# One decoder layer in split float32: cache copies in pieces, Sqrt for the inverse roots, sigmoids at another place, and all twelve heads of q in one pass over x

## The chip, the cores and the metric

The kernel runs on one core of a Trainium2 chip, as one launch. The metric is device time in microseconds (us); lower is better. TensorE (PE in the profile) multiplies matrices, ScalarE (ACT) and VectorE (DVE) do elementwise work, GpSimd (POOL) does a little of both and issues some DMAs, and SyncE (SP) issues most DMAs. Each engine works through its own instructions in order; they meet at semaphores.

## The reference, cut to what matters

One layer of a decoder for 256 prompt tokens and 8 decoded tokens (264 columns in all), width 2048, all in float32:

```python
xn = rmsnorm(x, norm_mix_g)
z  = xn @ w_in              # u, v (768 each), q (12 heads x 64), k, v (4 x 64 each), qm (512), 3 gates x 2048
o_g = gelu(u) * gmlp_spatial(rmsnorm(gelu(v)))            # causal 128x128 mixing
o_a = sliding_window_attention(q, k, v, cache_k, cache_v) # window 128, ALiBi, sinks
o_m = memory_attention(qm, mem_k, mem_v)                  # 256 memory tokens
x = x + (sig(g0)*(o_g @ w_br_g) + sig(g1)*(o_a @ w_br_a) + sig(g2)*(o_m @ w_br_m)) @ w_out
h = causal_conv3(rmsnorm(x, norm_ffn_g) @ w_up)
x = x + (gelu(h_a) * h_b) @ w_down
y = rmsnorm(x, final_norm_g)
# also returned: the windows of keys and values, shifted by one row for the 8 decoded tokens
# (new row 127 computed, rows 0..126 copied from cache rows 1..127), memory k and v, states
```

## The kernel before

**Arithmetic.** Every float32 matrix product is made of three matmuls in a faster format: the operand x is split into `xhi` and `xlo`, each weight tile into `whi` (a cast on ACT) and `wlo` (raw minus `whi`, on DVE), and `whi*xhi + whi*xlo + wlo*xhi` is summed in PSUM. Everything is kept transposed: features on the 128 partitions, the 264 tokens along the free axis. So one matmul streams 264 columns, and the kernel has over 11,000 of them.

**Chunks.** A weight matrix is read in chunks of 256 rows (two blocks of 128) by up to 512 columns. `wload` issues the DMA on SP into a tile `raw` (four buffers), `split` makes `whi` and `wlo` (six buffers each, so three chunks), `gemm` lists the chunks as items, and `run` walks the list: it splits one chunk ahead for the first four and two ahead afterwards, then lets the item issue its matmuls. An accumulator `acc` is one PSUM bank, four of the eight banks; the other four (`mis`) serve everything else.

**Slots.** `pump` is called once per six matmuls and advances `clock`; `at(slot, fn)` and `later(n, fn)` place other work (transposes, attention, norms) at a slot of that clock. `plan` lays out the attention, the memory attention, the gMLP branch and the convolution's state by slots counted from its start (`p(slot, ...)`). `InOrder` ties each engine's instructions into the order in which they are recorded, so this order is what an engine executes.

**The start.** x is loaded as eight tiles `xl` (two feature blocks of 128 each). `x_parts` transposes one pair of blocks on TensorE: per block two 128x128 transposes of prompt rows and one small one of the 8 decoded rows `xs`; then `xhi` on ACT and `xlo` on DVE, scaled by the norm's gain `gT`. `x_kept` keeps the plain x (`xT`) and squares; on POOL the squares are added up into `ssum`. The q columns of `w_in` come in two passes: heads 0 to 5 (three accumulators, 384 columns, 8 chunks, a pair of x transposed in each), then heads 6 to 11 (the same 8 pairs of x again). Between them `x_norm` makes the row norm: `token_norm` sums over the partitions (`ntp`), `inv_sqrt` does the root as Exp(-0.5 Ln v) with one Newton step, `spread` puts the result back along the free axis by a diagonal tile `dg` and matmuls (`stp`). The results, `r_bc`, scale each accumulator as it is read out (`r_evac`).

**The middle.** After q come k and v of the window attention, qm, the memory's keys and values (`macc`), u, v, and the gates; `plan` starts after k and v. In it `swa_plan` ends with `kv_shift`, which issues on POOL three DRAM to DRAM copies: the convolution's state, and the shifted rows of the two window caches, 1016 KB each, as one DMA each. `mem_plan` has the softmax of the memory attention (tiles `p_`, `mpT`) and for the 8 decoded tokens products on POOL (`mvc` times `pTs`). `gates` applies Sigmoid two slots after each pair of accumulators. `gmlp_plan` has the Gelus and a root.

**Activation tables.** Before an ACT function that the loaded table does not hold, an ACT_TABLE_LOAD stands in ACT's order. In the kernel before there are 16. The last stands in the final norm, between Ln and Exp.

**The end.** After the last `w_down` chunk the final norm's sums are taken (`nt`), `inv_sqrt` gives `ry`, and the rows of y, already transposed, are scaled and stored.

Of the kernel before, what the change touches and what calls it, by code (L numbers as in the profile page):

```python
# [60 lines left out]
def body(ctx, tc, x_prompt, x_sample, cache_swa_k, cache_swa_v, cache_mem_k, cache_mem_v, state_conv,  # L61
# [13 lines left out]
    psM = ctx.enter_context(tc.tile_pool(name="psM", bufs=4, space=PSUM))  # L75
# [4 lines left out]
    def mis_t(name="mis"):  # L80
        return psM.tile([128, 512], F32, name=name, tag="mis")
# [22 lines left out]
    def inv_sqrt(dst, v, shape):  # L104

        y = sm.tile(shape, F32, name="rs_y", tag="rs_y%d" % shape[1], bufs=2)
        t = sm.tile(shape, F32, name="rs_t", tag="rs_t%d" % shape[1], bufs=2)

        def a():
            S.activation(y, v, AF.Ln)  # L110
            S.activation(y, y, AF.Exp, scale=-0.5)

        def b():
            V.scalar_tensor_tensor(out=t, in0=y, scalar=-0.5, in1=y, op0=mul_, op1=mul_)
            V.tensor_tensor(t, t, v, op=mul_)
            V.scalar_tensor_tensor(out=dst, in0=t, scalar=1.5, in1=y, op0=add_, op1=mul_)
        return a, b

    def token_norm(srcs, out):

        st = {}

        def a():
            tp = st["tp"] = mis_t("ntp")
            for tb in range(3):
                np_ = 128 if tb < 2 else 8
                for i, q in enumerate(srcs):
                    T.matmul(tp[:np_, tb:tb + 1], lhsT=q[:, 128 * tb:128 * tb + np_], rhs=ones[:, 0:1],
                             start=i == 0, stop=i == len(srcs) - 1)
            v = st["v"] = sm.tile([128, 3], F32, name="nv_", tag="nv_", bufs=2)  # L130
            G.memset(v, 1.0)

        def b():
            tp, v = st["tp"], st["v"]
            V.tensor_scalar(v[:, 0:2], tp[:, 0:2], 1.0 / D, EPS, op0=mul_, op1=add_)
            V.tensor_scalar(v[:8, 2:3], tp[:8, 2:3], 1.0 / D, EPS, op0=mul_, op1=add_)
            st["f"] = inv_sqrt(out, v, [128, 3])
            st["f"][0]()
        return a, b, lambda: st["f"][1]()

    def spread(r, dst):

        st = {}

        def a():
            dg = st["dg"] = sm.tile([128, NT], F32, name="dg", tag="sq", bufs=4)
            V.tensor_scalar(dg[:, 0:128], ident, r[:, 0:1], None, op0=mul_)
            V.tensor_scalar(dg[:, 128:256], ident, r[:, 1:2], None, op0=mul_)
            V.tensor_scalar(dg[:8, 256:264], ident[:8, :8], r[:8, 2:3], None, op0=mul_)

        def b():
            tp, dg = mis_t("stp"), st["dg"]
            T.matmul(tp[:, 0:256], lhsT=ones, rhs=dg[:, 0:256], start=True, stop=True)
            T.matmul(tp[:, 256:264], lhsT=ones[:8, :], rhs=dg[:8, 256:264], start=True, stop=True)
            V.tensor_copy(dst, tp[:, :NT])
        return a, b


    ident = cst.tile([128, 128], F32, name="ident")
    make_identity(nc, ident)  # L160
    ones = cst.tile([128, 128], F32, name="ones")
    G.memset(ones, 1.0)
    warm = cst.tile([128, 1], F32, name="warm")
    S.activation(warm, ones[:, 0:1], AF.Ln)
# [10 lines left out]
    rx = cst.tile([128, 3], F32, name="rx")  # L175
# [5 lines left out]
    R, M, held = {}, {}, {}  # L181
    st_ld, st_mix, st_pb, st_me, st_gt, st_s2, st_s2p, st_s3k, st_s3v, st_s1, st_s5, st_mg = (
        ExitStack() for _ in range(12))


    ld = st_ld.enter_context(tc.tile_pool(name="ld", bufs=1))
    xls = [ld.tile([128, 2, 256], F32, name="xl%d" % i) for i in range(8)]
    xs = ld.tile([8, D], F32, name="xs")
    gm = ld.tile([16, 128], F32, name="gm")
    grow = ld.tile([48, 128], F32, name="grow")  # L190

    def x_load(i):
# [8 lines left out]
    def x_parts(k0):  # L201

        if k0 == 0:
            tp = mis_t("gtp")
            T.transpose(out=tp[:, 0:16], in_=gm, identity=ident[:16, :16])
            V.tensor_copy(gT[:, 0:16], tp[:, 0:16])
        xl = xls[k0 // 2]
        tps = []
        for j in range(2):
            kb = k0 + j  # L210
            tp = mis_t("xtp")
            js = slice(128 * j, 128 * j + 128)
            T.transpose(out=tp[:, 0:128], in_=xl[:, 0, js], identity=ident)
            T.transpose(out=tp[:, 128:256], in_=xl[:, 1, js], identity=ident)
            T.transpose(out=tp[:, 256:264], in_=xs[:, 128 * kb:128 * kb + 128], identity=ident[:8, :8])
            tps.append(tp[:, :NT])
        for j in range(2):
            S.activation(xhi[:, k0 + j, :], tps[j], AF.Copy, scale=gT[:, k0 + j:k0 + j + 1])
        for j in range(2):
            V.scalar_tensor_tensor(out=xlo[:, k0 + j, :], in0=tps[j], scalar=gT[:, k0 + j:k0 + j + 1],  # L220
                                   in1=xhi[:, k0 + j, :], op0=mul_, op1=sub_)
        return tps

    def x_kept(k0, tps):
        S.copy(xT[:, k0, :], tps[0])
        V.tensor_copy(xT[:, k0 + 1, :], tps[1])
        sq = [sm.tile([128, NT], F32, name="sq", tag="sq", bufs=4) if k0 + j else ssum for j in range(2)]
        S.activation(sq[0], tps[0], AF.Square)
        if k0 < KB - 2:
            G.tensor_tensor(sq[1], xT[:, k0 + 1, :], xT[:, k0 + 1, :], op=mul_)  # L230
        else:
            S.activation(sq[1], tps[1], AF.Square)
        E = G if k0 < KB - 2 else V
        if k0:
            E.tensor_tensor(ssum, ssum, sq[0], op=add_)
        E.tensor_tensor(ssum, ssum, sq[1], op=add_)

    def x_pair(k0):
        if k0 < KB:
            x_kept(k0, x_parts(k0))  # L240
# [12 lines left out]
    def split(load, n, pairs):  # L253
# [11 lines left out]
        for r, h, l in vs:  # L265
            S.copy(h, r)
        for r, h, l in vs:
            V.tensor_tensor(l, r, h, op=sub_)
        return list(zip(his, los))

    def run():
        chunks = [i for i, it in enumerate(items) if it[0]]
        ws, nxt, pos = {}, 0, 0
        for i, (sp, fn) in enumerate(items):
# [3 lines left out]
            look = pos + (0 if pos == 0 else 1 if pos < 4 else 2)  # L278
            while nxt < len(chunks) and nxt <= look:
                if nxt == 0:  # L280
                    wake = mis_t("wake")
                    for _ in range(5):
                        T.matmul(wake[:, 0:128], lhsT=ones, rhs=ones, start=True, stop=True)
                    x_load(0)
                    held["x"] = x_parts(0)
                    for _ in range(3):
                        T.matmul(wake[:, 0:128], lhsT=ones, rhs=ones, start=True, stop=True)
                ws[chunks[nxt]] = split(*items[chunks[nxt]][0])
                nxt += 1
                if nxt < 8:  # L290
                    x_load(nxt)
# [6 lines left out]
    def gemm(load, nkb, nm, ab, evac, pairs=False, pre=None, mid=None, banks=None):  # L298
# [3 lines left out]
        def chunk(kc):  # L302
            def mm(ws):
                if pre:
                    pre(kc)
                if kc == 0:
                    st["acc"] = banks() if banks else [acc_t() for _ in range(nm)]
                ahi, alo = ab()
                for m in range(nm):
# [9 lines left out]
                    if mid and m == 0:  # L319
                        mid(kc)  # L320
# [33 lines left out]


    def pre_q0(kc):
        if kc == 0:
            x_kept(0, held.pop("x"))
            x_pair(2)

    def open_mix():
        st_ld.close()
        R["mix"] = st_mix.enter_context(tc.tile_pool(name="mix", bufs=1))
        pb = st_pb.enter_context(tc.tile_pool(name="pb", bufs=1))
        R["kvT"] = pb.tile([128, 4, NT], F32, name="kvT")
        R["mkT"] = pb.tile([128, 4, 256], F32, name="mkT")
        R["mv_tm"] = pb.tile([128, 2, 512], F32, name="mv_tm")
        f6("qT")
        for m in range(3):
            r_evac("qT", 0, QS)(m, held[m])  # L370

    def x_norm():
        a, b, c = token_norm([ssum], rx)
        d, e = spread(rx, r_bc)
        later(1, a)
        later(2, b)
        later(5, c)
        later(5, d)
        later(8, e)
        later(9, gains)  # L380
        later(10, open_mix)

    gemm(wload(win, 1536, 384), KB, 3, xab, held.__setitem__, pairs=True, pre=pre_q0,
         mid=lambda kc: kc and x_pair(2 * kc + 2))
    act(x_norm)
    gemm(wload(win, 1536 + 384, 384), KB, 3, xab, r_evac("qT", 3, QS), pairs=True,
         banks=lambda: [acc_t(), mis_t("acc_"), mis_t("acc_")])
# [34 lines left out]
    def pre_m(kc):  # L422
# [5 lines left out]
        if kc == 6:  # L428
# [78 lines left out]

    def plan():
# [1061 lines left out]
```

## Time and profile before

| | |
|---|---|
| time, median of 3 runs | 1536.22 us (1534.65 to 1537.34) |
| the profiled execution's own time | 1537.49 us |
| its span, first to last instruction | 1535.8 us |
| busy: PE, DVE, ACT, POOL | 1512.8, 1008.1, 771.0, 156.5 us |
| mean granted TensorE clock | 0.995 of full |
| DMA | 285.82 MB, mean 186 GB/s |

Read it from PE down: PE is busy for nearly the whole span, and its busy time counts a matmul from its start to its modelled end, so that two that overlap cover the time once. A stretch in which matmuls start further apart than in the steady part is therefore the thing to look for, as well as PE's idle time. In the trace most instructions carry line L50, the helper that records them; tiles tell them apart. "xN" merges N alike instructions, and a float32 matmul counts as two.

### The profile page before, as it was taken

What the parts mean: (1) busy time and instruction counts of PE and PEld (TensorE: products, weight loads), DVE (VectorE), ACT (ScalarE), POOL (GpSimd) and SP (SyncE); (2) the same over time, 40 slices, a digit from 0 to 9 for tenths busy, and PEclk for the clock granted to TensorE, in tenths of its full rate; (3) what the DMA queues carried; (4) which work ended last, traced back from release to release, by engine and by line L of the source; (5) the groups of instructions that cost most, each with busy time, mean ns of one, the idle gap of its engine ahead of it and who ended that gap; (6) DMA issues with size and microseconds to landing.
All of it is one profiled execution on the core that took longest, in us unless ns stands there. A gap on an engine that the chain in (4) does not pass through costs nothing.

```text
span 1535.8 us, 31462 instructions
## 1 busy us (share of the span) xinstructions
PE 1512.8 (99%) x12118; PEld 1486.1 (97%) x12118; DVE 1008.1 (66%) x1926; ACT 771.0 (50%) x1481; POOL 156.5 (10%) x247
## 2 busy tenths in 40 slices
PE   9999998999999999999999999999999999999996
PEld 8997898899999999999999999999999999999996
DVE  7577695767565655766577777775444777777564
ACT  6467643556444444455555555554333555555443
POOL 5122241310000000001100000002000000000120
PEclk9999999999999999999999999999999999999998
DMA  6746697665566665555666666656556666665553
GB/s 192 220 154 206 202 315 259 200 193 178 166 183 184 183 180 179 180 180 170 185 180 179 181 184 183 180 180 186 180 183 182 183 179 179 180 179 186 179 165 109
DMA packets 154914, 285.82 MB, mean 186 GB/s; under 512 B 12140, under 2 KB 30380, under 8 KB 154716
## 3 DMA queue, kind: packets, MB, share of 16 engines
q1 hardware_dynamic: 151804, 276.30, 59.1%
q0 software_dynamic: 2960, 7.52, 1.8%
q8 instruction: 95, 1.56, 0.4%
q14 instruction: 55, 0.45, 0.1%
HBM read 279.36 MB, written 6.82 MB: 186 GB/s over the span
## 4 chain that ended last, share of the span: by engine, by line
PE 95%; DMA 2%; DVE 1%; ACT 1%; issue 1%; SPq 0%; POOLq 0%; POOL 0%; DVEq 0%; ACTq 0%
PE acc L50 87%; PE macc L50 3%; DMA raw<-in_w_in_dram 1%; PE xtp L50 1%; DVE wlo L50 1%; DMA k<-in_cache_swa_k_dram 0%; PE acc__552 L50 0%; PE acc__551 L50 0%; PE sps L50 0%; PE ov L50 0%; PE msov L50 0%; PE ptp L50 0%; ACT whi L50 0%; PE mtp L50 0%; PE ytp L50 0%
## 5 line engine op out<-in xcount | busy, mean ns | idle before, releaser
L50 DVE TENSOR_TENSOR wlo<-raw,whi 128x512 fp32r<-128x512 f32 (+1 forms) x1008 | 660.1, 697 | 478.4 <-ACT whi L50 476.2
L50 ACT CAST whi<-raw 128x512 fp32r<-128x512 f32 (+1 forms) x1008 | 564.2, 607 | 609.8 <-PE acc L50 400.2
L50 PE MATMUL acc<-xg_hi,whi 128*128 128x264 f32 x1408 | 400.4, 284 | 0.0
L50 PE MATMUL acc<-xg_lo,whi 128*128 128x264 f32 x1408 | 400.2, 284 | 0.0
L50 PE MATMUL acc<-xg_hi,wlo 128*128 128x264 f32 x1408 | 400.1, 284 | 0.0
L50 PE MATMUL acc<-xhi,whi 128*128 128x264 f32 x1152 | 337.2, 293 | 6.1 <-DVE vT L50 6.0
L50 PE MATMUL acc<-xlo,whi 128*128 128x264 f32 x1152 | 329.8, 286 | 0.4 <-DVE xlo L50 0.4
L50 PE MATMUL acc<-xhi,wlo 128*128 128x264 f32 x1152 | 329.8, 286 | 0.0
L50 PEld LDWEIGHTS acc<-xg_hi,whi 128*128 128x128 f32 x1408 | 265.5, 189 | 0.1
L50 PEld LDWEIGHTS acc<-xg_lo,whi 128*128 128x128 f32 x1408 | 265.0, 188 | 0.0
L50 PEld LDWEIGHTS acc<-xg_hi,wlo 128*128 128x128 f32 x1408 | 264.4, 188 | 0.0
L50 PEld LDWEIGHTS acc<-xhi,whi 128*128 128x128 f32 x1152 | 219.4, 190 | 10.2 <-DVE vT L50 6.2
L50 PEld LDWEIGHTS acc<-xlo,whi 128*128 128x128 f32 x1152 | 219.2, 190 | 1.3 <-DVE xlo L50 0.7
L50 PEld LDWEIGHTS acc<-xhi,wlo 128*128 128x128 f32 x1152 | 218.7, 190 | 0.2
L50 PE MATMUL acc<-ahi,whi 128*128 128x264 f32 x704 | 200.7, 285 | 0.0
L50 PE MATMUL acc<-ahi,wlo 128*128 128x264 f32 x704 | 200.1, 284 | 0.0
L50 PE MATMUL acc<-alo,whi 128*128 128x264 f32 x704 | 200.1, 284 | 0.0
L50 PEld LDWEIGHTS acc<-ahi,whi 128*128 128x128 f32 x704 | 132.7, 189 | 0.0
L50 PEld LDWEIGHTS acc<-alo,whi 128*128 128x128 f32 x704 | 132.6, 188 | 0.0
L50 PEld LDWEIGHTS acc<-ahi,wlo 128*128 128x128 f32 x704 | 132.2, 188 | 0.0
L50 DVE SCALAR_TENSOR_TENSOR t<-H,cvT,t 128x256 f32<-128x256 f32 x176 | 84.7, 481 | 3.1
L50 POOL TENSOR_TENSOR ssum<-ssum,sq 128x264 f32<-128x264 f32 x41 | 35.8, 873 | 461.8 <-ACT sq L50 459.6
(339 smaller groups left out, 1703.6 us busy)
## 6 DMA issues: line engine op xcount, KB each, us to landing
raw<-in_w_up_dram SPq DMA_DIRECT2D x176, 512.0 KB
raw<-in_w_in_dram SPq DMA_DIRECT2D x112, 512.0 KB
raw<-in_w_down_dram SPq DMA_DIRECT2D x88, 512.0 KB
raw<-in_w_in_dram SPq DMA_DIRECT2D x48, 384.0 KB
raw<-in_w_out_dram SPq DMA_DIRECT2D x32, 512.0 KB
raw<-in_w_mem_kv_dram SPq DMA_DIRECT2D x16, 512.0 KB
raw<-in_w_br_g_dram SPq DMA_DIRECT2D x12, 512.0 KB
raw<-in_w_br_a_dram SPq DMA_DIRECT2D x48, 128.0 KB
```

Of the source, the lines that this page charges most:

```text
L50: r = f(*a, **k)
```

## The change

In words, part by part:

- **q in one pass.** `q_chunk` takes all twelve heads in one walk over the pairs of x: per pair two chunks of 384 columns, six accumulators (four of `acc`, two of a pool `psX` whose other two banks serve `mis`); after q, `psX` is closed and `psM` with four banks opened. The first four half-chunks go block by block, each operand part for three heads in a row, the rest as before. The accumulators are read out on ACT with no norm; `q_norm` multiplies by `r_bc` on DVE at slots 82 and 84.
- **The start.** The 8 decoded rows are loaded as 128 rows of 128 elements (on ACT's DMA queue, like the gain `gm`) and transposed by one 128x128 transpose; a pair of x then needs four transposes and no small ones. Seven matmuls on `ones` stand first instead of five. `x_start` orders the first casts by hand; `x_pair(i)` stands at slot 5i-3.
- **Squares by fours.** `x_squares` squares four blocks in one ACT instruction and adds them on DVE in pairs; POOL adds nothing there any more.
- **Norms.** `token_norm` sums with one matmul of `ones` against `ssum` (264 columns), which leaves the sum on every partition; `spread` is gone. Roots are Sqrt on ACT, then a reciprocal on DVE and the same Newton step.
- **Cache copies.** `kv_shift` copies one cache of one decoded token, 127 KB; 16 of them stand from slot 222 to 357, nine slots apart. The state's copy stands at slot 216.
- **Sigmoids.** Those of the first group of gates stand at slots 322 to 337 of the plan, among those of the second group, after the Gelus.
- **Small shifts.** `mem_prep(0)` stands one chunk earlier, two score blocks 3 or 4 slots later, the decoded tokens' attention and memory softmax 4 slots later.

```diff
     def inv_sqrt(dst, v, shape):
         def a():
-            S.activation(y, v, AF.Ln)
-            S.activation(y, y, AF.Exp, scale=-0.5)
+            S.activation(y, v, AF.Sqrt)
         def b():
+            V.reciprocal(y, y)
             ...
+    def token_norm(src, dst):          # the old one and spread() are removed
+        def a():
+            tp = st["tp"] = mis_t("ntp")
+            T.matmul(tp[:, :NT], lhsT=ones, rhs=src, start=True, stop=True)
+        def b():
+            V.tensor_scalar(v, st["tp"][:, :NT], 1.0 / D, EPS, op0=mul_, op1=add_)
+            S.activation(dst, v, AF.Sqrt)
+        def c():
+            V.reciprocal(y, dst)
             ...
+    def x_pair(i):
+        tp = mis_t("xtp")
+        tps = [x_trans(tp[:, 256 * j:256 * j + 256], i, j) for j in range(2)]
+        for j in range(2):
+            x_hi(2 * i + j, tps[j])
+        S.copy(xT[:, 2 * i:2 * i + 2, NP_], tp.rearrange("p (j t) -> p j t", j=2))
+        for j in range(2):
+            x_lo(2 * i + j, tps[j])
+    def x_squares(g):
+        S.activation(sq, xT[:, 4 * g:4 * g + 4, :], AF.Square)
             ...
+    def q_chunk(kc, h):
+        parts = ((0, 0), (1, 0), (0, 1))
             ...
+            for w, g, m, j, (a, b) in todo:
+                o = qs["acc"][3 * g + m][:, :NT]
+                T.matmul(o, lhsT=blk(w[j][b], m), rhs=xab()[a][:, 2 * kc + j, :], start=..., stop=last)
+                if last:
+                    S.activation(R["qT"][:, 3 * g + m, :], o, AF.Copy, scale=QS)
+                if qs["n"] % 6 == 0:
+                    pump()
+    for i in range(1, 8):
+        at(5 * i - 3, lambda i=i: x_pair(i))
+    for g, slot in enumerate((14, 24, 34, 42)):
+        at(slot, lambda g=g: x_squares(g))
+    for slot, f in zip((50, 51, 54, 58), token_norm(ssum, r_bc)):
+        at(slot, f)
+    for h in range(2):
+        at(82 + 2 * h, lambda h=h: q_norm(h))
-        def kv_shift():
-            G.dma_start(o_cs[0, :, 0, :], state_conv[0, :, 1, :])
-            for src, dst in ((cache_swa_k, o_ks), (cache_swa_v, o_vs)):
-                G.dma_start(dst[0]..., src[0]...)          # 8 x 2 x 16256 elements
+        def kv_shift(src, dst, b):
+            G.dma_start(dst[0, b]..., src[0, b]...)        # 16 x 2032 elements
-        p(s + 72, kv_shift)
+        p(216, state_shift)
+        for k in range(8):
+            p(222 + 18 * k, kv_shift, cache_swa_k, o_ks, k)
+            p(231 + 18 * k, kv_shift, cache_swa_v, o_vs, k)
-                    later(2, lambda: S.activation(gt[...], gt[...], AF.Sigmoid))
+                    if gi == 0:
+                        at(plan_at[0] + 322 + 6 * br + 3 * (m // 2), sig)
+                    else:
+                        later(2, sig)
```

How the instructions stand, at three places. On PE, from its first instruction to the first product of q, before (`wake` are matmuls on `ones`, `xtp` transposes of x, `gtp` that of the gain, `acc` an accumulator):

```order
L50 MATMUL wake<-ones 128x128 x5
L50 MATMUL gtp<-ident,gm 128x16
L50 MATMUL xtp<-ident,xl_99 128x128 x2
L50 MATMUL xtp<-ident,xs 128x8
L50 MATMUL xtp<-ident,xl_99 128x128 x2
L50 MATMUL xtp<-ident,xs 128x8
L50 MATMUL wake<-ones 128x128 x3
L50 MATMUL xtp<-ident,xl_100 128x128 x2
L50 MATMUL xtp<-ident,xs 128x8
L50 MATMUL xtp<-ident,xl_100 128x128 x2
L50 MATMUL xtp<-ident,xs 128x8
L50 MATMUL acc<-xhi,whi 128x264
```

The same place in the changed kernel, up to the transposes of the second pair (`xstp` is that of the decoded rows, `xgtp` that of the gain):

```order
L50 MATMUL wake<-ones 128x128 x7
L50 MATMUL xstp<-ident,xs 128x128
L50 MATMUL xtp<-ident,xl_76 128x128 x2
L50 MATMUL xgtp<-ident,gm 128x128
L50 MATMUL xtp<-ident,xl_76 128x128 x2
L50 MATMUL wake<-ones 128x128 x3
L50 MATMUL acc<-xhi,whi 128x264 x3
L50 MATMUL acc<-xlo,whi 128x264 x3
L50 MATMUL acc<-xhi,wlo 128x264 x3
L50 MATMUL acc<-xhi,whi 128x264
L50 MATMUL acc__182<-xhi,whi 128x264
L50 MATMUL xtp<-ident,xl_77 128x128 x4
```

The second pair's transposes moved behind the first twelve products, and the small transposes are gone. On POOL, where the copies of the caches stood (- before, + changed; `mvc` are the products for the memory attention of the decoded tokens):

```order
 L50 DMA out_dram<-in_state_conv_dram 8x11264
-L50 DMA out_dram<-in_cache_swa_k_dram 8x2x16256
-L50 DMA out_dram<-in_cache_swa_v_dram 8x2x16256
 L50 MEMSET zf 128x135
 L50 MEMSET zf 128x1
-L50 TENSOR_TENSOR mvc<-mvc,pTs 128x512 x16
+L50 DMA out_dram<-in_cache_swa_k_dram 16x2032
+L50 TENSOR_TENSOR mvc<-mvc,pTs 128x512 x2
+L50 DMA out_dram<-in_cache_swa_v_dram 16x2032
+L50 TENSOR_TENSOR mvc<-mvc,pTs 128x512 x3
+L50 DMA out_dram<-in_cache_swa_k_dram 16x2032
+L50 TENSOR_TENSOR mvc<-mvc,pTs 128x512 x3
```

Two large copies ahead of the products became sixteen small ones, six of them ahead of or among the products and ten behind. On ACT, in the final norm:

```order
 L50 CAST whi<-raw 128x512 x10
 L50 ACTIVATE sq<-xT 128x264 x4
-L50 ACTIVATE rs_y<-nv__19663 128x3
-L50 ACT_TABLE_LOAD
-L50 ACTIVATE rs_y<-rs_y 128x3
+L50 ACTIVATE rs_y<-nv__19607 128x3
 L50 ACTIVATE y_tm<-y_tm,ry 128x512
```

The table load and one activation between the sums and the scaling of y are gone; over the kernel ACT has 10 table loads instead of 16.

## Rows read from the trace of the kernel before

**Rows 1.** The page's first part: busy us, share, instructions by engine.

```profile
PE 1512.8 (99%) x12118; PEld 1486.1 (97%) x12118; DVE 1008.1 (66%) x1926; ACT 771.0 (50%) x1481; POOL 156.5 (10%) x247
```

**Rows 2.** Windows: stretch, length, busy (count) by engine, PEclk, DMA share, GB/s.

```profile
240.00:250.00 10.00, 5.21 (x50) 4.26 (x48) 2.28 (x4) 1.29 (x3) 0.00 (x0) 1.00 0.90 328
250.00:260.00 10.00, 8.84 (x51) 8.84 (x52) 5.29 (x12) 3.87 (x10) 0.30 (x2) 0.66 0.63 197
...
280.00:290.00 10.00, 8.17 (x60) 7.51 (x60) 7.15 (x17) 6.50 (x14) 3.13 (x3) 1.00 0.49 152
290.00:300.00 10.00, 9.16 (x69) 8.71 (x69) 7.83 (x15) 6.86 (x14) 2.08 (x2) 1.00 0.63 197
...
400.00:450.00 50.00, 50.00 (x413) 50.00 (x412) 31.78 (x63) 21.95 (x40) 0.00 (x0) 1.00 0.59 181
```

**Rows 3.** Timeline of PE: start us, us, instruction, [idle before, releaser].

```profile
1.21 2.50 PE L50 MATMUL wake<-ones 128*128 128x128 f32 x10 [1.21 <-POOL ones L50]
...
6.05 1.65 PE L50 MATMUL wake<-ones 128*128 128x128 f32 x6
7.50 0.63 PE L50 MATMUL xtp<-ident,xl 128*128 128x128 f32 x2
...
9.08 0.59 PE L50 MATMUL acc<-xhi,whi 128*128 128x264 f32 x1
...
251.16 0.59 PE L50 MATMUL acc<-xhi,whi 128*128 128x264 f32 x1 [5.95 <-DVE vT L50]
```

**Rows 4.** The chain that ended last: start us, us, what.

```profile
9.15 5.58 PE acc L50 x24
...
18.07 0.90 PE xtp L50 x6
...
26.87 0.42 DVE wlo L50
...
37.41 0.46 PE ntp L50 x6
...
43.17 0.74 PE stp L50 x4
...
56.18 24.81 PE acc L50 x204
...
251.16 5.65 PE acc L50 x24
...
295.88 0.44 PE mptp L50 x4
...
758.63 0.94 PE stp L50 x4
```

**Rows 5.** Timeline of ACT, columns as for PE.

```profile
5.34 0.48 ACT L50 ACTIVATE xhi<-xtp,gT 128x264 fp32r<-128x264 f32 x1 [3.04 <-PE xtp L50]
...
6.56 0.92 ACT L50 CAST whi<-raw 128x384 fp32r<-128x384 f32 x2
...
248.82 1.14 ACT L50 CAST whi<-raw 128x512 fp32r<-128x512 f32 x2 [8.67 <-DMA raw<-in_w_in_dram]
...
289.90 1.28 ACT L50 ACT_TABLE_LOAD   x1 [1.04 <-DVE nm L50]
...
1524.41 1.28 ACT L50 ACT_TABLE_LOAD   x1
```

**Rows 6.** Timeline of DVE, columns as for PE.

```profile
24.04 3.25 DVE L50 TENSOR_TENSOR wlo<-raw,whi 128x384 fp32r<-128x384 f32 x4 [0.40 <-ACT whi L50]
...
40.55 1.03 DVE L50 TENSOR_TENSOR wlo<-raw,whi 128x384 fp32r<-128x384 f32 x2 [2.25 <-ACT whi L50]
```

**Rows 7.** DMA issues: what, engine, count, KB each, median us to landing.

```profile
out_dram<-in_cache_swa_k_dram POOLq DMA_DIRECT2D x1, 1016.0 KB, 11.1
```

**Rows 8.** Groups of instructions: busy us, mean ns of one, idle before.

```profile
L50 POOL TENSOR_TENSOR mvc<-mvc,pTs 128x512 f32<-128x512 f32 x16 | 18.3, 1154 | 39.4 <-DVE pTs L50 15.5 <-DMA mvc<-in_cache_mem_v_dram 14.8 <-DVE mvc L50 5.1
...
L50 POOL DMA_DIRECT2D out_dram<-in_cache_swa_k_dram x1 | 0.6, 598 | 0.0
```

More of the change, by code (lines that the diff above doesn't have):

```diff
@@ new lines, in token_norm @@
+        return a, b, c, d
+    st_ld = ExitStack()
+    ld = st_ld.enter_context(tc.tile_pool(name="ld", bufs=1, side="right"))
+    xls = [ld.tile([128, 2, 256], F32, name="xl%d" % i) for i in range(8)]
+    xs = ld.tile([128, 128], F32, name="xs")
+    gm = ld.tile([128, 128], F32, name="gm")
+    grow = ld.tile([48, 128], F32, name="grow")
+    part = ld.tile([128, 2, NT], F32, name="part")
+    ones = cst.tile([128, 128], F32, name="ones")
+    G.memset(ones, 1.0)
+    G.memset(gm, 0.0)
+    S.dma_start(xs, x_sample.rearrange("b o (k f) -> (b o k) f", f=128))
@@ L238, in x_pair, with x_trans, x_hi, x_lo @@
-    def x_pair(k0):
-        if k0 < KB:
-            x_kept(k0, x_parts(k0))
+    def x_trans(tp, i, j):
+        for t in range(2):
+            T.transpose(out=tp[:, 128 * t:128 * t + 128], in_=xls[i][:, t, 128 * j:128 * j + 128], identity=ident)
+        return tp
+    def x_hi(k, tp):
+        S.activation(xhi[:, k, NP_], tp, AF.Copy, scale=gT[:, k:k + 1])
+    def x_lo(k, tp):
+        V.scalar_tensor_tensor(out=xlo[:, k, NP_], in0=tp, scalar=gT[:, k:k + 1], in1=xhi[:, k, NP_],
+                               op0=mul_, op1=sub_)
@@ new lines, in x_pair, with x_start @@
+    def x_pair(i):
+        tp = mis_t("xtp")
+        tps = [x_trans(tp[:, 256 * j:256 * j + 256], i, j) for j in range(2)]
+        for j in range(2):
+            x_hi(2 * i + j, tps[j])
+        S.copy(xT[:, 2 * i:2 * i + 2, NP_], tp.rearrange("p (j t) -> p j t", j=2))
+        for j in range(2):
+            x_lo(2 * i + j, tps[j])
+    def x_start(loads):
+        wake = acc_t("wake")
+        for _ in range(7):
+            T.matmul(wake[:, 0:128], lhsT=ones, rhs=ones, start=True, stop=True)
+        tx, tg, t0, t1 = mis_t("xstp"), side_t("xgtp"), mis_t("xtp"), side_t("xtp")
+        T.transpose(out=tx[:, 0:128], in_=xs, identity=ident)
+        t0 = x_trans(t0[:, 0:256], 0, 0)
+        T.transpose(out=tg[:, 0:128], in_=gm, identity=ident)
+        t1 = x_trans(t1[:, 0:256], 0, 1)
+        for _ in range(3):
+            T.matmul(wake[:, 0:128], lhsT=ones, rhs=ones, start=True, stop=True)
+        rows = tx[:, 0:128].rearrange("p (b k) -> p k b", k=KB)
+        gx = ld.tile([128, KB, NS], F32, name="gx")
+        V.tensor_copy(gT[:, 0:16], tg[:, 0:16])
+        V.tensor_tensor(gx, rows, gT[:, 0:16].unsqueeze(2).to_broadcast([128, KB, NS]), op=mul_)
+        a, b = (split_tiles(load, n, pairs) for load, n, pairs in loads)
+        x_hi(0, t0)
+        S.copy(xhi[:, :, NS_], gx)
+        a[1](0)
+        x_hi(1, t1)
+        S.copy(xT[:, 1, NP_], t1)
+        b[1](0)
+        a[1](1)
+        b[1](1)
+        x_lo(0, t0)
+        V.tensor_tensor(xlo[:, :, NS_], gx, xhi[:, :, NS_], op=sub_)
+        a[2](0)
+        x_lo(1, t1)
+        b[2](0)
+        a[2](1)
+        V.tensor_copy(xT[:, :, NS_], rows)
+        b[2](1)
+        S.copy(xT[:, 0, NP_], t0)
+        return a[0], b[0]
@@ L306, in mm @@
                 if kc == 0:
[L307 removed]
+                    st["acc"] = [acc_t() for _ in range(nm)]
                 ahi, alo = ab()
@@ L372, in x_norm @@
[L372 to L387, printed above, removed]
+    R["mix"] = st_mix.enter_context(tc.tile_pool(name="mix", bufs=1))
```

210 lines of the change are left out of this document (89 added, 121 removed).

## Prediction

> **What bounds the kernel now.** I read the page's busy shares first: PE is busy for 1512.8 us of a span of 1535.8 [rows 1]. So the question is only where PE does not multiply, or multiplies slowly or for nothing. Then the windows. In the steady part 413 matmuls of 264 columns start in 50 us, 0.121 us each [rows 2]; two stretches fall out of it, 240 to 260 (PE busy 5.21 and 8.84 of 10 us, the granted clock 0.66 in the second) and 280 to 300 (8.17 and 9.16 of 10) [rows 2]. Last the timeline of PE and the chain that ended last, for the first 57 us, where PE counts as busy but much of it is transposes, and for the two norms and the end. The change touches just these places. From 400 to 1500 us the chain is nearly pure products, and no edit can gain there but at the second norm.
>
> **The change part by part.** Six terms carry the sum, made against the profiled execution, 1537.49 us; the median of the runs lies 1.27 below that.
>
> *A, the first product.* It starts at 9.08 us [rows 3]. What stands ahead of it on PE in the changed order: seven matmuls on `ones`, six transposes, three matmuls on `ones`. Three of these matmuls take 1.45 us (6.05 to 7.50), six transposes 1.58 (7.50 to 9.08) [rows 3]. `ones` is now filled before the identity and not after it, so PE starts some 0.1 us ahead of its 1.21 [rows 3]: 1.1 + 7 x 0.48 + 1.6 + 1.45 = 7.5. ACT's side is no later: the gain's transpose ends near 5.5; its copy and the cast of the decoded rows I put at 0.2 each, `xhi` takes 0.48, `whi` 0.46 (two in 0.92) [rows 5], together 6.9. The first weights were there by 6.56 [rows 5] and are now issued two DMAs sooner, so I expect no wait for them. Gain 1.6; bounds 0 (the decoded rows or the weights land as late as PE now begins) and 2.0.
>
> *B, transposes in the q pass.* After 9.15 the chain has six sets of about 0.90 us [rows 4], 5.4. Seven sets of four come in their place; four 128x128 transposes took 0.44 [rows 4], one set still at the low clock about twice that: 3.5. Gain 1.9; bounds 1.5 and 2.3.
>
> *C, two norms.* `ntp` 0.46 and `stp` 0.74 at the first, and 0.94 for `stp` at the second, with an `ntp` like the first [rows 4]: 2.6. One float32 matmul of 264 columns replaces each pair. Nothing like it stands in the trace; the nearest are `ntp` (three thin ones, 0.46) below and `stp` (256 and 8 columns, 0.94) above. I take 0.6, near the plain `stp`. Gain 1.4; bounds 0.7 and 1.7. The reciprocal of 264 columns has no row. It is off the path: from slot 54 to the first use of `r_bc` at slot 77 there are 23 slots of six matmuls, 16.7 us, and some 13 slots at the second norm. In DVE's order it delays the `wlo` behind it, which have a lead of two chunks, over 4 us.
>
> *D, waits in the q pass.* From 9.15 to 56.18 [rows 4] are 47.0 us: 288 products at 0.121 are 34.9, the first 24 at the low clock cost 5.58 instead of 2.9 [rows 4], 2.7 more; transposes 5.4, norm 1.2. The rest, 2.8, is waits and turnarounds, the longest for `wlo` at 26.87 [rows 4]. There four `wlo` took 3.25 us, 0.81 each, while POOL added squares; two later ones took 1.03, 0.52 each, without it [rows 6]. POOL's adds are gone. Per pair of x ACT then has four casts of 0.46, two `xhi` of 0.48, one copy and half a wide square: near 3.9 us for 36 products and a set of transposes, 4.8 us. DVE has four `wlo`, two `xlo` and its share of adds, near 3.7. Both fit, with little room. I take 1.9 for what is left of the 2.8. Gain 0.9; bounds -2.8 (as much again) and 2.3.
> For the low clock I keep 24 products, as many as both there and after the idle at 245 [rows 4].
>
> *E, the stall at 245 us.* PE idles 5.95 us [rows 3], and the 24 products after it take 5.65 [rows 4], 2.75 above the steady rate: 8.7. The chain behind it: the cast at 248.82 waited 8.67 us for its weights [rows 5]; the two copies of 1016 KB, issued near 237, land after 11 [rows 7], and the DMAs move 328 GB/s in 240 to 250 [rows 2]. A piece is an eighth of a copy, one in nine slots, 6.5 us: 127 KB in 6.5 us is 20 GB/s, beside 180 GB/s of weights [rows 2] and the loads of memory values. They begin in a stretch of 152 to 197 GB/s [rows 2]. An eighth of 11.1 us is 1.4 us of delay to a weight chunk, within the lead of two chunks. Gain 8.7; bounds 0 (the weights would be late without the copies) and 8.7. I take the upper end: the wait has the copies' length and begins with them.
>
> *F, tables at 280 to 300 us.* PE idles 1.83 + 0.84 = 2.7 us there [rows 2], while ACT loads a table between Sigmoid and Exp (289.90, one of three in 30 us) [rows 5]. No Sigmoid stands there any more, so no load. Gain 2.2; bounds 0 and 2.7. The moved Sigmoids, six of 528 columns (a cast of 512 took 0.57, two in 1.14 [rows 5]), join ACT at slots 322 to 337; their first reader is the first branch, after slot 384.
>
> *G, the end.* One load of 1.28 us stands at 1524.41 [rows 5] between the sums and the scaling of y, where no engine has anything else. It goes; an Exp goes and a reciprocal of three columns comes, which I let cancel. Gain 1.3; bounds 1.0 and 1.4.
> The Trainium skill ("ScalarE: Activation LUTs", "Table sets: the hidden batching unit") says that Ln and Exp share a set, so that going from one to the other needs no load. By that rule there would be nothing to gain here. The trace disagrees: the load stands there and takes 1.28 us.
>
> The rest I cost at nothing, with its cover: the read-out of q on ACT (six of near 0.5 us while the first k and v chunks run; the bank needed first is free a chunk early), `q_norm` on DVE (four slots before the scores), the shifts by 3 or 4 slots, `mem_prep` a chunk earlier (bounds -0.5 and 0.5). The first loads of the convolution's state, on POOL, now wait for the room of x and land about 10 us later, still 20 us ahead of their use.
>
> Sum: 1.6 + 1.9 + 1.4 + 0.9 + 8.7 + 2.2 + 1.3 = 18.0. 1537.5 - 18.0 = 1519.5; less the 1.3 to the median, **1518.2 us**.
>
> **The rivals.** *R1, the q pass is fed too slowly.* Its 6.3 MB of weights and 2.1 MB of x have to come in about 42 us, 200 GB/s, where the steady part draws 181 [rows 2]. For it: the pass loses its slack, two chunks now come per pair. Against it: 328 GB/s in 240 to 250 [rows 2]. At 181 GB/s the 8.4 MB take 46.4 us, 4.4 more: 1522.6.
>
> *R2, the pieces still stop PE.* Sixteen POOL issues instead of two; six stand ahead of or among the `mvc` products, and DVE, which adds these products in its order, makes `wlo` too. An issue takes 0.60 us, a product 1.15 [rows 8]; per nine slots POOL has three products and one issue, 4.1 of 6.5 us, so it does not back up. If the pieces cost half of E, 1522.6 again.
> The Trainium skill ("SBUF — State Buffer", "SBUF: two separate sides") speaks against small DMAs from POOL: while VectorE runs an operation on two ports, GpSimd cannot write the descriptors. Its figures, 620 ns alone and 3100 ns beside such an operation, would make POOL's load, by an estimate, 6.6 of 6.5 us. The trace's issue of 0.60 us shows no such delay, so it moves little of my chance.
>
> *R3, the change doesn't remove the stall*, because the weights were late anyway: caches of both attentions are loaded in the same stretch, and these loads stay. Against it: without the copies' 2 MB, 6 us of traffic at 328 GB/s [rows 2] are gone, as much as PE's idle time. E is then 0: 1526.9.
>
> *R4, slower.* The clock stays low in the q pass, because waits there keep PE from the unbroken work after which it rose both times [rows 4]. A product then costs 0.235 instead of 0.121 us: 264 of them (288 less 24) cost 30 us more, 1548. It decides from 158 products on (18.0 / 0.114). Against it: before, with waits in the same pass, the clock rose after 24 and stayed.
>
> **How the numbers follow.** Forecast 0.64, with a range of its own from 1513 to 1523; R1 0.13, R2 0.10, R3 0.07, R4 0.03, and 0.03 for no difference, if several terms fail at once. The upper ends of all bounds give 2.0 + 2.3 + 1.7 + 2.3 + 8.7 + 2.7 + 1.4 = 21.1, 1515.1; a clock that rises at once would give 2.7 more. So 1512 to 1527, which holds R1, R2 and R3 at their prices and leaves out R4 and what several lower ends together would give. About 0.2%, 3 us, is what a measurement of this kernel can tell from no change. Faster 0.94 (forecast and R1 to R3), the same 0.03, slower 0.03.
>
> **What would show it.** A: the first product near 7.5 us. B to D: k and v begin near 50 us instead of 56, with four transposes in 0.44 us and `wlo` at 0.52. C: no `stp`. E: no idle time of PE above 1 us near 235 to 245, the clock there unbroken, pieces landing in a few us. F: no table load between the memory attention's Exps. G: 1.3 us less from the last sum to the first store. I am wrong if PE waits for `raw` or `wlo` several times in the q pass, if a stall of several us stands between 220 and 400 us again, or if the granted clock falls below full there.

## The result, and the profile after

The changed kernel takes 1516.43 us (median of four runs, 1515.19 to 1519.66) where the kernel before takes 1536.48 in the same series: the ratio is 0.9869, with a 95% interval of 0.9856 to 0.9883, or 20.05 us less. The forecast was 1518.2. The profiled execution is 1516.01 us long, its span 1514.3, 21.5 below the span of before.

The page's first part of after, which answers to [rows 1]:

```profile
PE 1500.1 (99%) x12091; PEld 1477.4 (98%) x12091; DVE 1008.6 (67%) x1918; ACT 766.3 (51%) x1473; POOL 149.5 (10%) x240
```

Then the windows (stretch, length, busy time and count by engine, granted clock, DMA share, GB/s), against [rows 2]:

```profile
240.00:250.00 10.00, 10.00 (x84) 9.98 (x84) 5.38 (x13) 4.12 (x10) 0.84 (x3) 1.00 0.75 235
250.00:260.00 10.00, 10.00 (x78) 9.61 (x77) 6.38 (x15) 5.44 (x15) 1.47 (x2) 1.00 0.81 243
260.00:270.00 10.00, 9.75 (x70) 8.99 (x68) 9.16 (x15) 3.36 (x11) 6.62 (x7) 1.00 0.45 135
...
290.00:300.00 10.00, 9.15 (x72) 8.69 (x71) 8.74 (x13) 4.43 (x8) 5.78 (x6) 1.00 0.71 240
400.00:450.00 50.00, 50.00 (x413) 50.00 (x412) 32.18 (x64) 23.07 (x43) 0.00 (x0) 1.00 0.62 184
```

The stall is gone and the granted clock is full in all of these windows, but three of the ten-microsecond windows from 260 to 300 still have some idle time of PE. The steady rate is what it was: 413 products in 50 us. The timeline of PE, against [rows 3]:

```profile
1.07 3.36 PE L50 MATMUL wake<-ones 128*128 128x128 f32 x14 [1.07 <-POOL ones L50]
...
5.50 0.93 PE L50 MATMUL wake<-ones 128*128 128x128 f32 x6
6.65 0.63 PE L50 MATMUL acc<-xhi,whi 128*128 128x264 f32 x3 [0.22 <-ACT whi L50]
...
8.80 0.67 PE L50 MATMUL xtp<-ident,xl 128*128 128x128 f32 x4 [0.43 <-ACT xT L50]
...
46.22 0.28 PE L50 MATMUL acc<-xhi,whi 128*128 128x264 f32 x1
```

The first product starts at 6.65 us (9.08 before), and the first product of k and v at 46.22 (56.02 before). Three wakes (six instructions) take 0.93 us where they took 1.65, and products stand 0.12 us apart from the first one on: the clock is full at 5.5 us, where before had the low level, 1.2 GHz (products 0.22 us apart), until 14.3. The column of the granted clock can't show this: the trace's record of it begins only when it is full, at 14.73 us in before and at 5.69 in after, and the windows take it as 1.00 ahead of that. That 0.22 us is the low level is seen after the stall in before: there the products stand as far apart, and the clock reads 0.50 from 251 to 257 us. The chain that ended last (the work that each later step had to wait for, followed back from the end), against [rows 4], with a set of four transposes and the two norms:

```profile
22.01 0.44 PE xtp L50 x4
...
47.83 0.45 PE ntp L50 x2
...
734.01 0.45 PE ntp L50 x2
```

No `stp` is left. The end on ACT, against the last of [rows 5], and a group of `wlo` on DVE, against [rows 6]:

```profile
1504.03 0.20 ACT L50 ACTIVATE rs_y<-nv__19607 128x3 f32<-128x3 f32 x1 [1.17 <-DVE nv__19607 L50]
1505.06 0.72 ACT L50 ACTIVATE y_tm<-y_tm,ry 128x512 f32<-128x512 f32 x1 [0.83 <-DVE ry L50]
```

```profile
19.81 1.95 DVE L50 TENSOR_TENSOR wlo<-raw,whi 128x384 fp32r<-128x384 f32 x4
```

Four `wlo` take 1.95 us, 0.49 each, in place of 0.81. Last the pieces as DMA issues (KB each, median us to landing), against [rows 7], and the groups of POOL, against [rows 8]:

```profile
out_dram<-in_cache_swa_k_dram POOLq DMA_DIRECT2D x8, 127.0 KB, 4.1
```

```profile
L50 POOL TENSOR_TENSOR mvc<-mvc,pTs 128x512 f32<-128x512 f32 x16 | 20.1, 1264 | 34.1 <-DMA mvc<-in_cache_mem_v_dram 14.9 <-DVE pTs L50 14.8 <-DVE p__3953 L50 1.5
L50 POOL DMA_DIRECT2D out_dram<-in_cache_swa_k_dram x8 | 4.1, 515 | 0.6 <-issue 0.4
```

If I lay the two timelines of PE side by side by the number of products done, the lead grows like this: 2.4 us at the first product, 9.8 at the first of k and v, 9.0 at the first of `qmT`, 18.9 after 2400 products (near 400 us), then 1.3 more at the second norm and 1.3 at the end.

### The profile page after: what moved, and what is told of

The parts are those of the page before. It is cut to its first block, busy times and chain, and to the rows that moved or that the text cites. A ratio compares the mean times of both kernels' runs of the same rounds, so it can differ in the third digit from the quotient of the medians.

```text
span 1514.3 us, 31382 instructions
## 1 busy us (share of the span) xinstructions
PE 1500.1 (99%) x12091; PEld 1477.4 (98%) x12091; DVE 1008.6 (67%) x1918; ACT 766.3 (51%) x1473; POOL 149.5 (10%) x240
## 4 chain that ended last, share of the span: by engine, by line
PE 94%; DMA 2%; DVE 2%; ACT 1%; issue 1%; POOL 0%; POOLq 0%; DVEq 0%; SPq 0%; ACTq 0%
PE acc L50 87%; PE macc L50 3%; DMA raw<-in_w_in_dram 2%; DVE wlo L50 1%; ACT whi L50 0%; PE acc__182 L50 0%; PE acc__183 L50 0%; DMA sinkc<-in_attn_sinks_dram 0%; PE ov L50 0%; PE msov L50 0%; PE xtp L50 0%; PE sps L50 0%; PE wake L50 0%; PE ptp L50 0%; PE ytp L50 0%
## 5 line engine op out<-in xcount | busy, mean ns | idle before, releaser
L50 PEld LDWEIGHTS acc<-xg_hi,whi 128*128 128x128 f32 x1408 | 265.5, 189 | 0.0
L50 PE MATMUL acc<-mghi,whi 128*128 128x264 f32 x256 | 72.8, 284 | 0.0
```

The source lines that it names most:

```text
L50: r = f(*a, **k)
```

## The experiments

Twelve kernels ran. Names in b_ are the kernel before with one edit, names in a_ the kernel after with one edit. Two cautions go with all of them. The kernel after was timed in the first series only, and before's median moved by 0.7 us between the series, so a difference of 1 to 3 us from after is not a sure one. And the profiled executions differ by up to 4 us near 200 to 230 us (the DMAs' share is 0.81 to 1.03 there in after), even where the edit acts only later: a_nocopy, whose order is that of after up to 243 us, is 1.3 us behind after there.

**The two halves of the change.** *b_rest* is before with everything but the new front.

```
-                    later(2, lambda: S.activation(gt[:, m - 1:m + 1, :], ..., AF.Sigmoid))
+                    (the moved sigmoids, as in the change)
-        p(s + 72, kv_shift)
+        (the sixteen pieces, as in the change)
-            S.activation(y, v, AF.Ln); S.activation(y, y, AF.Exp, scale=-0.5)
+            S.activation(y, v, AF.Sqrt); V.reciprocal(y, y)
```

> The kernel before with the cache copies in pieces, Sqrt and reciprocal for the roots, the twelve-slot shifts of the plan and the late sigmoids, and without the new front (first products, q pass, norms by one product stay as before). Theory: the front is worth the 9.0 us that stand between the traces at the first product of the qm pass and the second norm 0.8 more, and nothing of it is given back: 1516.4 + 9.8 = 1526.2 us. Rival: an earlier front only comes sooner to the same loads, and part of its gain is lost again before 250 us; then 1520 to 1524 us. By the prediction's own terms (front 5.0, second norm 0.8) it would be 1522.2 us.

Measured: 1525.70 us (1525.21 to 1526.01), ratio 0.9928 [0.9914, 0.9941]; before took 1537.19 in that series. The theory holds. The front and the second norm are worth 1525.70 - 1516.43 = 9.3 us, and what lies behind the front (E, F, G, and the small shifts of slots) 1537.19 - 1525.70 = 11.5. The front's gain isn't given back: between the traces it is 9.2 us at k and v, 8.1 at 400 us, and 9.2 again behind the second norm.

**The copies.** *b_pieces* cuts them in before, *b_nocopy* leaves them out there, *a_onecopy* puts them back whole into after, *a_nocopy* leaves them out.

```
 b_pieces:   -        p(s + 72, kv_shift)
             +        for k in range(8):
             +            p(222 + 18 * k, kv_shift, cache_swa_k, o_ks, k)
             +            p(231 + 18 * k, kv_shift, cache_swa_v, o_vs, k)
 a_onecopy:  the reverse;  b_nocopy, a_nocopy: neither
```

> The kernel before with only its cache copies in 16 pieces. Theory: the whole stall goes: 1536.5 - 8.7 = 1527.8 us, and no wait for whi or raw over 0.5 us between 240 and 400 us. Rival R2 of the prediction, pieces still hold weight loads: 1530 to 1533 us. Rival R3, the stall is not from the copies: 1536.5 us.

> The kernel before without the two cache copies (it leaves out the same rows). Theory: what the copies cost there is 7.0 us, all of it taken away by the pieces: 1529.6 us like b_pieces. By the prediction's term E: 1536.6 - 8.7 = 1527.9 us. Rival: the pieces cost 2 us or more: below 1527.6 us.

> The kernel after with the two cache copies as one DMA each at their old place, the rest as it is. Theory: the stall of the products at 251.16 us in the kernel before came from these two 1016 KB copies alone; it comes back with the 8.7 us that the prediction gave it: 1525.1 us, PE busy below 2 us in its worst 10 us. Rival: the earlier front and the other order of weight loads take part of the stall away by themselves; then 1518 to 1522 us.

> The kernel after without the two cache copies (it leaves out 127 of 128 rows of the two shifted caches). Theory: the pieces cost nothing that PE shows, 1516.4 us, give or take 1. Rival R2 of the prediction: sixteen issues and their traffic still cost part of the 8.7 us; then 1512 to 1515 us.

Measured: b_pieces 1529.61 us (1529.15 to 1532.37), ratio 0.9950 [0.9937, 0.9963]; b_nocopy 1529.27, ratio 0.9951 [0.9937, 0.9965]. In before the pieces cost nothing that a time shows, and the copies there cost 7.0 us by b_pieces (1536.61 before in its series) and 7.8 by b_nocopy (1537.08): R3 is out, and R2 at its price too. The 8.7 isn't: it lies within both intervals, and in the traces the stretch of the stall alone, from the 1200th to the 1300th product, is 8.8 us shorter in b_pieces and in b_nocopy than in before, with no idle time of PE from 230 to 270 us. Both of these executions, the longest of their runs, lost 3 us or more on before ahead of it, near 200 to 230 us. a_onecopy takes 1521.22 us (1520.13 to 1521.39), ratio 0.9894 [0.9881, 0.9907], 4.8 above after: the rival's range, so in the new order the whole copies cost only about half of 8.7. a_nocopy takes 1515.25, its four runs within 0.2 us of one another, while those of after reach from 1515.19 to 1519.66: the pieces cost nothing in the best execution, and 1.2 us at the median.

Why are the same two copies worth 8.7 us in one trace and less in another? ACT's casts of weights in before, ahead of the stall and at it, with the idle time before them in brackets:

```profile
235.28 0.93 ACT L50 CAST whi<-raw 128x384 fp32r<-128x384 f32 x2 [4.98 <-DMA raw<-in_w_in_dram]
...
239.02 1.14 ACT L50 CAST whi<-raw 128x512 fp32r<-128x512 f32 x2 [0.39 <-PE acc L50]
```

and the same in a_onecopy:

```profile
228.43 0.93 ACT L50 CAST whi<-raw 128x384 fp32r<-128x384 f32 x2 [0.44 <-PE acc L50]
237.54 1.14 ACT L50 CAST whi<-raw 128x512 fp32r<-128x512 f32 x2 [8.18 <-DMA raw<-in_w_in_dram]
```

In both ACT waits more than 8 us for the chunk behind the copies. But in before a chunk at 235.28 had already been waited for 4.98 us, so the lead was used up when the copies were issued (236.64), and PE idled 5.95 us. In a_onecopy the copies were issued at 226.39, and there was some lead left (at 228.43 ACT waited for PE, not for a DMA). PE idled only this, and then had the granted clock at 0.50 for 3.4 us:

```profile
238.21 0.39 PE L50 MATMUL acc<-xhi,whi 128*128 128x264 f32 x1 [2.76 <-ACT whi L50]
```

What had taken the lead in before, I didn't test. It wasn't the copies: without them, in b_nocopy, ACT still waits 2.58 us for the same chunk, at 236.53. That the lead makes the difference is read from one trace of each order.

**The clock at the start.** *a_wake5* takes two of the seven wakes away; *b_wake* gives before seven, and `ones` ahead of the identity; *b_rest_wake* does the same to b_rest.

```
-        for _ in range(7):          (a_wake5; the reverse in b_wake and b_rest_wake)
+        for _ in range(5):
             T.matmul(wake[:, 0:128], lhsT=ones, rhs=ones, start=True, stop=True)
```

> The kernel after with 5 wake products ahead of the first transposes instead of 7 (10 instead of 14 instructions). Theory: the full granted clock from the first product on came because TensorE worked from 1.07 us on without a hole; with two fewer it stands idle from about 3.5 to 4.2 us, the wakes at 5.5 us run at 1.2 GHz again (about 1.6 us in place of 0.93), the products stand 0.22 us apart for some us, and the kernel takes 1519 to 1520 us, 2.5 to 3.5 more than 1516.4. Rival: the clock rose early for a reason that has nothing to do with the wakes; then 1515.8 to 1516.5 us and the first product near 6.65 us.

> The kernel before with ones set ahead of the identity and 7 wake products instead of 5, nothing else. Theory: the hole at 3.71 us closes, the clock is full at the wakes of 6 us and the 24 products after 9.08 us stand 0.12 instead of 0.22 us apart: 2.5 to 3.3 us less, 1533.2 to 1534.0 us, unless conversions then keep the products waiting. Rival: the clock does not answer to this; the wakes end 0.4 us later and the kernel takes 1536.5 to 1537 us.

> The kernel b_rest with ones set first and 7 wake products in place of 5. Theory: in the kernel before this edit brought k and v forward by 2.43 us (b_wake), and the stall of the copies hid it in the time; here no stall follows, so it shows: 1525.7 - 2.4 = 1523.3 us, products 0.12 us apart from the first on. Rival: waits for weights between 200 and 290 us take the gain back whatever comes before them; 1525 to 1526 us.

PE in a_wake5:

```profile
1.07 2.50 PE L50 MATMUL wake<-ones 128*128 128x128 f32 x10 [1.07 <-POOL ones L50]
3.98 0.44 PE L50 MATMUL xstp<-ident,xs 128*128 128x128 f32 x1 [0.41 <-DMA xs<-in_x_sample_dram]
...
5.61 1.49 PE L50 MATMUL wake<-ones 128*128 128x128 f32 x6
6.92 1.03 PE L50 MATMUL acc<-xhi,whi 128*128 128x264 f32 x3
```

and in b_wake:

```profile
1.07 3.36 PE L50 MATMUL wake<-ones 128*128 128x128 f32 x14 [1.07 <-POOL ones L50]
4.35 0.28 PE L50 MATMUL gtp<-ident,gm 16*128 16x16 f32 x1
...
7.90 0.39 PE L50 MATMUL acc<-xhi,whi 128*128 128x264 f32 x1
8.12 0.28 PE L50 MATMUL acc<-xlo,whi 128*128 128x264 f32 x1
8.24 0.28 PE L50 MATMUL acc<-xhi,wlo 128*128 128x264 f32 x1
```

The clock answers to the edit, both ways. With five wakes (and PE idle for 0.41 us before 3.98) three wakes take 1.49 us, and products stand 0.22 us apart until 9.7 us (the record of the full clock begins at 9.88); with seven and no hole, in b_wake, products are 0.12 us apart from 8.12 on (the record begins at 5.31), where before has 0.22 until 14.3. Whether it is the hole or the work of the two wakes, these runs don't separate: each edit changes both. In b_wake the first product comes 1.18 us sooner and k and v 2.43 sooner (53.59 for 56.02); the other 1.2 is won in the first 24 products.

The times say less. a_wake5 takes 1518.77 us (ratio 0.9883 [0.9870, 0.9895]), 2.3 above after. Its trace, 1.6 above, shows 0.95 of this before k and v, and two more waits near 207 and 218 us (0.30 for `wlo`, and 0.79 for a bank that DVE reads) that after doesn't have. In after a slower start costs less than in before, because there PE waits 0.43 us for `xT` at 8.80 once it is fast. b_wake takes 1535.82 (0.9992 [0.9982, 1.0002]), 0.8 below before, which is no difference. b_rest_wake takes 1525.61 (1523.33 to 1529.18), the same as b_rest, though its one profiled execution, 1523.68, keeps 1.5 of its 1.8 us at k and v. So the early clock is shown, and its worth at the end, between 0 and 2.4 us, isn't settled.

**Sigmoids and roots.** *a_sig* puts the sigmoids of the first gates back; *a_lnexp* has Ln and Exp again in the short norms.

```
 a_sig:    -                    if gi == 0: at(plan_at[0] + 322 + 6 * br + 3 * (m // 2), sig)
           +                    later(2, sig)
 a_lnexp:  -            S.activation(y, v, AF.Sqrt); V.reciprocal(y, y)
           +            S.activation(y, v, AF.Ln); S.activation(y, y, AF.Exp, scale=-0.5)
```

> The kernel after with the sigmoids of the first gate group back beside the softmax of the memory attention. By the prediction's term F it takes 2.2 us more: 1518.6 us. Theory from the trace of after: the table loads are gone but mov and msov still wait 1.3 us for other reasons, so the move gave about 1.1: 1517.5 us, with Sigmoid and Exp table loads of 1.28 us between 255 and 285 us back in the trace. Rival: the waits there come from VectorE alone; 1516.4 us.

> The kernel after with the roots of the two short norms by Ln and Exp again (the long ones keep Sqrt), the last preload of a table Ln. Theory: the table load of 1.28 us between Ln and Exp stands in the tail again, which nothing covers, and the reciprocal of 0.18 us goes: 1.2 to 1.4 us more, 1517.7 us, with nothing else changed. Rival: the tail is bound by the output transfers, and the time stays at 1516.4 us.

a_sig takes 1519.05 us (1518.16 to 1519.52), 2.6 above after, a difference that the intervals of the two ratios (0.9883 [0.9869, 0.9896] here) don't keep apart. In its one trace 1.7 of 3.5 us are lost by 230 us, ahead of the first moved sigmoid (263.8), and 1.8 behind it. The prediction's 2.2 lies between these, nearer than my later 1.1. The table loads stand there again, and PE waits 1.7 us for ACT's `mpT` where it waits 0.5 in after:

```profile
270.53 1.28 ACT L50 ACT_TABLE_LOAD   x1 [1.99 <-DVE nm L50]
```

```profile
PE mov L50 <- ACT mpT L50: 1.7, 1, 1.7
```

a_lnexp has the load back in the end of ACT's timeline:

```profile
1503.98 0.20 ACT L50 ACTIVATE rs_y<-nv__19607 128x3 f32<-128x3 f32 x1 [1.17 <-DVE nv__19607 L50]
1504.21 1.28 ACT L50 ACT_TABLE_LOAD   x1
1505.50 0.20 ACT L50 ACTIVATE rs_y<-rs_y 128x3 f32<-128x3 f32 x1
1506.32 0.72 ACT L50 ACTIVATE y_tm<-y_tm,ry 128x512 f32<-128x512 f32 x1 [0.62 <-DVE ry L50]
```

From the root to the scaling of y are 2.34 us; in after 1.03 (1504.03 to 1505.06). That is 1.3. Its profiled execution is 1517.33 us, 1.3 above that of after; its runs (median 1519.40, 1517.33 to 1522.02) spread too far for a finer statement.

**What is still open at 260 to 300 us.** *a_ez* moves one copy from DVE to ACT; *a_lead* does that and loads the memory values eight slots earlier.

```
-            V.tensor_copy(A["ez"], A["zf"])
+            S.copy(A["ez"], A["zf"])
-            p(b + 14 + 3 * u, v_load, u)            (a_lead only)
+            p(b + 6 + 3 * u, v_load, u)
```

> The kernel after with the copy of zf into ez on ScalarE in place of VectorE (one instruction). Theory: this copy of 128x135 took 2.49 us on VectorE while GpSimd multiplied, and VectorE's next work, the rows that p__3777 and mpT wait for, came late by that; without it the waits of 0.25 us at 265.5 and 0.45 us at 270.5 us go: 1515.5 to 1516.0 us. Rival: VectorE's next operations are held by GpSimd's products in its place; no change, 1516.4 us.

> The kernel a_ez with the loads of the memory values eight slots earlier (GpSimd's products waited for them). Theory: GpSimd's products then run in even steps, vlo is there when msov wants it, and the wait of 0.85 us at 296 us goes too: 1515.0 to 1515.6 us. Rival: the earlier loads collide with the weights near 250 us and a chunk comes late; 1517 us or more.

a_ez takes 1516.16 us (1514.24 to 1520.30): not to be told from after. Its profiled execution no longer has the two waits at 265.5 and 270.5, and is 1.8 us shorter than that of after. a_lead takes 1522.45 (1521.13 to 1523.92), 6 us more, the time that its rival expected. PE stops twice in it. The first stop, with DVE and POOL beside it:

```profile
257.29 0.62 DVE L50 TENSOR_SCALAR p__3694<-p__3694,den 128x256 f32<-128x256 f32 x2
...
261.87 1.10 DVE L50 TENSOR_TENSOR gt<-acc,r_bc 128x264 f32<-128x264 f32 x3
...
263.07 5.58 DVE L50 TENSOR_SCALAR p__3781<-p__3781,den 128x256 f32<-128x256 f32 x2
```

```profile
261.91 3.04 POOL L50 TENSOR_TENSOR mvc<-mvc,pTs 128x512 f32<-128x512 f32 x3
264.90 0.54 POOL L50 DMA_DIRECT2D out_dram<-in_cache_swa_k_dram  x1
265.46 3.04 POOL L50 TENSOR_TENSOR mvc<-mvc,pTs 128x512 f32<-128x512 f32 x3
```

```profile
268.71 0.55 PE L50 MATMUL mptp<-ident,p__3781 128*128 128x128 f32 x3 [2.94 <-DVE p__3781 L50]
```

The same two scalings of `p` take 0.62 us while POOL rests, and 5.58 while it multiplies; they end when POOL's groups of three end. PE waits 2.94 us for them. With its first data there in time POOL worked six products with hardly a pause, and DVE's scalings waited for longer.

The second stop is the larger one, and there the rival was right in part: weights are late, if not near 250 us. The tile `mvc` has eight buffers, and the ninth load, eight slots earlier in SyncE's order than in after, has to wait for one of them (14.2 us, for DVE's sum of `mvc`); the weights behind it in that order wait too. The first row gives the waits in sum, their number and the longest:

```profile
SPq L50 <- DVE mvc L50: 18.8, 2, 14.2
```

```profile
261.98 0.38 SPq L50 DMA_DIRECT2D raw<-in_w_in_dram  x1
276.60 0.33 SPq L50 DMA_DIRECT2D mvc<-in_cache_mem_v_dram  x1
277.02 0.39 SPq L50 DMA_DIRECT2D raw<-in_w_in_dram  x1
```

```profile
292.05 1.14 ACT L50 CAST whi<-raw 128x512 fp32r<-128x512 f32 x2 [3.65 <-DMA raw<-in_w_in_dram]
```

```profile
299.81 0.50 PE L50 MATMUL msov<-vlo,ez 128*128 128x512 f32 x1 [2.77 <-DVE vlo L50]
```

```profile
300.00:310.00 10.00, 10.00 (x68) 9.86 (x68) 6.71 (x13) 3.53 (x6) 3.33 (x5) 0.83 0.91 339
```

In after the longest wait of this kind is 1.8 us, three weight loads are issued between 262 and 277 us, and ACT waits for none of them from 260 to 300. In a_lead the `vlo` comes behind the late chunk in DVE's order, PE stops 2.77 us for it, and then the granted clock is 0.50 from 301.3 to 304.8. By the number of products done, the first stop costs 1.7 us against after, and the second, with the low clock, 3.3; all of this is read from the one trace of a_lead. No version that beats after by more than a measurement can tell came out of this.

## Why the prediction came out as it did

The sign and the mechanisms were right, and 1518.2 is 1.8 us above the measured time; the sum, 18.0, is 2 us below the 20.05. But A to D, which the prediction put at 5.8, measured 9.3 (after against b_rest), a miss of 3.5 that three of the four terms share by lying above the bounds given for them; E to G, put at 12.2, measured 11.5 (b_rest against before). That the whole comes out so near is in part luck: the second miss takes away from the first, and the halves add up to 20.8, not 20.05, because before's median moved between the series.

*A, 1.6:* 2.4 in the traces. The failed step is two durations: I took three wakes at 1.45 us, which is their time at 1.2 GHz, and they ran at 2.4 in 0.93; and I took the six transposes at 1.58 from [rows 3], and they took 1.28 (4.22 to 5.50). ACT was no later than worked out (0.22 us of waiting for `whi` at 6.65), and the weights were there.

*B, 1.9:* about 3.5, the largest miss. A set cost PE more than the chain showed before, and less after. From the start of a set to the start of the product behind it, the six sets of before cost 6.1 us in sum (I had 5.4) and the seven of after 2.5 (I had 3.5). The chain's pieces are one engine's stretch and leave out what a change of work costs at its ends; the start times of the neighbours have it all.

*C, 1.4:* 2.4, 1.1 at the first norm (by start times 1.38 us became 0.25) and 1.3 at the second (the lead grows from 18.9 to 20.2 there; the chain's pieces, 0.46 + 0.94 for 0.45, give only 0.95). The one product of 264 columns has 0.45 us on the chain, not the 0.6 that I took. The unseen reciprocal took 1.79 us for 264 columns and delayed nothing, as argued.

*D, 0.9:* 1.9 up to the first product of qm (what is left of the 9.0 there), of which b_wake's trace gives 1.2 to the clock. The step that failed is the sentence that keeps 24 products at the low clock: in after none ran there. The price I had put on it, 2.7, wasn't far off (2.43 at k and v in b_wake), but I had it as a remark on the range and not as a case: the order showed seven wakes in place of five, and the trace of before a hole of 0.5 us behind the five, up to 4.22 us. The waits that I left in the pass, 1.9, are 1.1 (0.6 ahead of the transposes at 8.80, 0.5 for a `wlo` ahead of the product at 20.41). These four make 10.2 against the trace of before; against b_rest's they are 9.2, as b_rest is 0.6 us ahead of before at k and v (the record of its full clock begins at 13.66).

*E, 8.7:* 7.0 to 7.8 by itself in before, 4.8 in after. It was read right from the one profile: the stretch of the stall gives 8.8 in two traces, and the stall went whole. What it is worth in time depends on the order, by the traces on the lead that the weights have at that moment. My lower bound, that the weights would be late without the copies, isn't borne out: in b_nocopy a cast still waits 2.58 us for its weights, but PE doesn't stop there.

*F, 2.2:* 1.8 (in a_sig's trace) to 2.6 (by its time). *G, 1.3:* 1.3 (a_lnexp, its trace). E to G together fell 0.7 short of 12.2, which is no more than the noise. The Trainium skill's table in "ScalarE: Activation LUTs", section "Table sets: the hidden batching unit", by which Ln to Exp needs no load, has the trace against it a second time: a_lnexp shows the load of 1.28 us between them.

*The rivals.* R1: in the q pass neither ACT nor PE waits for a load of weights. R2: the pieces land in 4.1 us, and cost 0 (b_nocopy) to 1.2 us (a_nocopy). R3: fell with b_pieces. R4: the clock rose sooner instead of later.

## What to carry to other kernels

Put a price on a step from the start times of what stands before and behind it, at the clock that will hold there, not from the lengths in the chain. Ask of each stretch at the low clock what PE did before it: here two more wakes, which also closed a hole of half a microsecond, brought the full clock from 14.7 to 5.3 us. When you ask what a large transfer costs a stream, look at the lead that the stream has at that moment, at how late the chunk before it was. And a load that is placed early but must wait for a buffer holds up all that stand behind it on its engine: 14.2 us in a_lead.

## What the runs showed of the hardware that I had not expected

In these traces VectorE's work with its source and its result in SBUF waits for GpSimd's products, and not only for the one under way. In a_lead one scaling of 128x256 took 2.04 us and the next 3.62, against 0.31 without GpSimd; in after the cast of `zf` to `ez`, 128x135, took 2.49 us, while the operations with a source in PSUM around it kept to 0.4 each:

```profile
261.48 0.76 DVE L50 TENSOR_TENSOR gt<-acc,r_bc 128x264 f32<-128x264 f32 x2
262.16 2.49 DVE L50 CAST ez<-zf 128x135 fp32r<-128x135 f32 x1
264.58 0.42 DVE L50 TENSOR_TENSOR gt<-acc,r_bc 128x264 f32<-128x264 f32 x1
```

The Trainium skill ("SBUF — State Buffer", section "SBUF: two separate sides") says that of an operation of VectorE on two ports and one of GpSimd the first to start holds the pair of ports they share for the whole instruction, and the other is fully blocked. The traces agree on the block. They show it longer than one instruction: 3.62 us beside three products of together 3.04. In the prediction I weighed this page for the other direction, VectorE holding up GpSimd's issues, and there 0.51 us for an issue shows nothing of it.

A reciprocal on VectorE is dear by its width: 1.79 us for 128x264 in after, where those of 128x2 take 0.15 to 0.17.
